# A hybrid encoder layer: transposes of the normalisation moved behind the state update, S5 regrouped, GLU second in the tail

## The chip, the cores and the metric

One Trainium2 chip, of which one core is used. The time is the device time of one launch in microseconds (us). The core has five engines, each with its own queue of instructions that it works off in order: TensorE (PE, matmuls and transposes, with a loader for weights, PEld), VectorE (DVE), ScalarE (ACT), GpSimd (POOL) and SyncE (SP), which here issues the DMAs. Matmuls write into PSUM, which has eight banks; the other engines empty them into SBUF.

## The reference

One layer over 1,152 rows (1,024 of a prompt, and 8 streams of 16 new rows) of 1,024 columns. A single projection feeds four branches, which are gated, projected, merged, projected again and normalised.

```python
def trunk_layer(x, p, rel_bias, st):
    h = split_cols(x @ p['w_in'])
    ya = s5_branch(h['a_u'], p, st)       # 32 groups, 64 complex states each; GELU, then GLU
    yb = dsa_branch(h, rel_bias, st)      # top-k attention
    yc = gdn_branch(h, p, st)             # gated DeltaNet
    yd = gla_branch(h, p, st)             # gated linear attention
    branches = stack(y_i * silu(gate_i))
    proj = einsum('ntbw,bwd->ntbd', branches, p['w_branch'])
    mixed = sum(sigmoid(merge) * proj) @ p['w_out']
    return layer_norm(DN_ALPHA * x + mixed)

def gdn_block_step(s, xs):                # one chunk of 64 rows
    ...                                   # v_new by a triangular solve, from k, v, beta, s
    o = exp(gc) * (q @ s) + (q @ k.T * dec) @ v_new
    s = exp(g_last) * s + (k * exp(g_last - gc)).T @ v_new
    return s, o                           # then rms_norm(o) * norm

def s5_branch(u, p, st):
    ...                                   # h_t = a * h_(t-1) + B u_t, complex
    y = real(C h_t) + d * u
    g = gelu(y) @ p['s5_w_glu']
    return g[..., :512] * sigmoid(g[..., 512:])
```

## The kernel before

The rows are worked on in nine tiles of 128 (tile 8 is the eight streams). Projections run in three passes of 32-bit matmuls per product (`mm3`, L189 to L191), 128 x 384 outputs at a time; their outputs are named `pg` (the input projection, its `merge` columns among them), `mix` (a branch's output projection), `glu` and `fin`. DeltaNet (`gdn_tile`) and GLA (`gla_scan`) carry a state S from tile to tile. In a DeltaNet tile the order is: triangular blocks `m`, `u`, `x` through ScalarE and VectorE, `kq`, the products `ks` and `qs` with the state, `vn`, `oi`; then `o` is normalised (`rms_gate`: squares on ScalarE, a Newton root on VectorE, `o` scaled at L1063), transposed on TensorE into `py` (L1066), gated and stored; then the state update `S` (L1025, added at L1030).

S5 goes in eight parts of four groups (`s5_part`). A part builds its matrices on VectorE (`bs`, `cs`, `AB` L1541 to L1543, `OM`), multiplies (`im`, `sx`, `kk`), fills the step matrix `TD` by DMA through DRAM, rotates (`cross`, L1584, half on VectorE and half on GpSimd), scans (L1589), writes the states `HS`, steps the eight sample streams (L1603 to L1608), multiplies again (`s5y`, L1617 and L1618), applies GELU and stores.

The tail runs the branches' `mix` in the order b, c, GLU, a, d, then `fin`. Of branches' inputs (`yl`, split into YH and YL by L112 and L113) four tiles exist; the GLU keeps two gate tiles (`glgt`, L1734).

The order on every engine is static. A list scheduler sets it when the kernel is built, from its own cost model and from priorities: recurrent chains, loads of branch inputs and the like are recorded as urgent, projections and `mix` as filler, and filler goes where an urgent instruction isn't ready by the scheduler's reckoning. `TensorE` then works this order off strictly. PSUM is in three pools: `pg` with 2 banks, `pn` with 2, and `pm` with 4, from which `m`, `u`, `kq`, `ks`, `qs`, `vn`, `oi`, `py` and `S` take theirs in turn.

## Time and profile before

| | |
|---|---|
| median of 3 runs | 1908.05 us (1903.02 to 1910.44) |
| profiled execution | 1909.76 us, span 1908.0 us |
| mean granted clock of TensorE | 0.982 of full |
| busy: TensorE, VectorE, ScalarE, GpSimd | 95%, 76%, 35%, 14% |
| attention, and DeltaNet's preparation beside S5 parts 0 and 1 | 0 to 1055 us |
| DeltaNet tiles 0 to 7 | 1055 to 1278 us |
| sample tile, rest of S5, GLA's decays | 1278 to 1420 us |
| GLA | 1420 to 1675 us |
| rest of GLU, mix of a and d | 1675 to 1800 us |
| `fin` and layer norm | 1800 to 1908 us |

Busy shares are over the whole span. A stretch is read by its own row: its busy time, and the waits of TensorE in it, by the line that waited and what released it. The profiled execution is 1.7 us above the median.

### The profile page before, as it was taken

The page shows a single profiled execution, that of the slowest core. Times are in us where ns is not written, and L with a number is a line of the kernel's source. Part 1 is how long each engine was busy: PE and PEld are TensorE (multiplying, and loading weights), DVE is VectorE, ACT ScalarE, POOL GpSimd, SP SyncE. Part 2 cuts the span into 40 slices and gives each one's busy share as a digit, 9 for nine tenths or more (in the row PEclk, how much of TensorE's full clock was granted, in tenths as well). Part 3 has the DMA queues.
Part 4 walks back from the last instruction along what each step waited for, and adds up shares of the span by engine and source line. Part 5 has one row for each costly group of instructions (what it writes and reads, how often), then busy time and mean ns, then how long its engine had stood idle before and what let it go on. Part 6 is the DMA issues. An engine that isn't in the chain of part 4 may idle for free.

```text
span 1908.0 us, 31158 instructions
## 1 busy us (share of the span) xinstructions
PE 1804.6 (95%) x10962; PEld 1710.1 (90%) x10962; DVE 1447.6 (76%) x3914; ACT 670.9 (35%) x1535; POOL 270.9 (14%) x297
## 2 busy tenths in 40 slices
PE   8999999999999999998989989899898999979997
PEld 7989999999989999997889888888888998979986
DVE  6289999944999997368890279976657899857776
ACT  4261211233666656245321333332373233222200
POOL 1110222111222210101211112211232000000000
PEclk9999999999999999999999899999999999989999
DMA  6322322232323212467335545444455673376422
GB/s 192 99 67 74 89 90 84 90 101 86 96 75 84 69 55 67 115 214 232 102 96 136 160 134 144 139 134 128 123 166 166 188 173 104 109 229 188 143 88 89
DMA packets 345290, 234.54 MB, mean 123 GB/s; under 512 B 82891, under 2 KB 327419, under 8 KB 345134
## 3 DMA queue, kind: packets, MB, share of 16 engines
q1 hardware_dynamic: 337262, 220.88, 40.1%
q10 hardware_dynamic: 7488, 10.62, 1.5%
q8 instruction: 87, 1.43, 0.3%
q0 software_dynamic: 384, 1.05, 0.2%
q14 instruction: 69, 0.57, 0.1%
HBM read 156.12 MB, written 76.35 MB: 122 GB/s over the span
## 4 chain that ended last, share of the span: by engine, by line
PE 39%; DVE 13%; DMA 5%; issue 3%; ACT 2%; POOL 1%; SPq 1%; DVEq 0%; POOLq 0%; ACTq 0%
PE pg L190 4%; PE pg L191 4%; PE pg L189 4%; PE mix L189 3%; PE mix L190 3%; PE mix L191 3%; PE fin L191 2%; PE fin L190 2%; PE fin L189 2%; PE lv L1209 1%; PE glu L191 1%; PE glu L190 1%; PE glu L189 1%; DMA S<-in_state_gdn 1%; DVE pb L870 1%
## 5 line engine op out<-in xcount | busy, mean ns | idle before, releaser
L189 PE MATMUL pg<-XH,whi 128*128 128x384 f32 x1648 | 564.0, 342 | 0.9 <-DVE gth L238 0.9
L190 PE MATMUL pg<-XL,whi 128*128 128x384 f32 x1648 | 564.3, 342 | 0.0
L191 PE MATMUL pg<-XH,wlo 128*128 128x384 f32 x1648 | 563.4, 342 | 0.0
L189 PEld LDWEIGHTS pg<-XH,whi 128*128 128x128 f32 x1648 | 312.7, 190 | 5.2 <-issue 1.8
L191 PEld LDWEIGHTS pg<-XH,wlo 128*128 128x128 f32 x1648 | 312.5, 190 | 4.1 <-issue 2.0
L190 PEld LDWEIGHTS pg<-XL,whi 128*128 128x128 f32 x1648 | 312.6, 190 | 3.1 <-issue 1.1
L109 ACT CAST whi<-wst 128x1024 fp32r<-128x1024 f32 (+2 forms) x121 | 109.5, 907 | 253.6 <-PE pg L190 118.1
L110 POOL TENSOR_TENSOR wlo<-wst,whi 128x1024 fp32r<-128x1024 f32 x44 | 109.6, 2492 | 335.3 <-ACT whi L109 329.6
L189 PE MATMUL mix<-YH,whi 128*128 128x384 f32 x384 | 132.7, 347 | 13.1 <-ACT YH L112 9.4
L110 DVE TENSOR_TENSOR wlo<-wst,whi 128x512 fp32r<-128x512 f32 (+2 forms) x77 | 76.4, 993 | 77.5 <-ACT whi L109 76.6
L190 PE MATMUL mix<-YL,whi 128*128 128x384 f32 x384 | 131.9, 344 | 1.1 <-DVE YL L113 1.1
L191 PE MATMUL mix<-YH,wlo 128*128 128x384 f32 x384 | 131.9, 344 | 0.0
L1684 ACT ACTIVATE mth<-pg 128x384 f32<-128x384 f32 x96 | 46.7, 487 | 138.3 <-PE pg L191 95.6
L392 DVE TENSOR_SCALAR_CACHE_REDUCE tkj<-mk,tk_c 128x384 bf16<-128x384 f32 (+6 forms) x112 | 90.9, 875 | 0.6
L392 DVE TENSOR_SCALAR_CACHE_REDUCE tkj<-tkh,tk_c 128x384 bf16<-128x384 bf16 (+6 forms) x112 | 90.9, 876 | 0.5
L189 PEld LDWEIGHTS mix<-YH,whi 128*128 128x128 f32 x384 | 73.4, 192 | 15.2 <-ACT YH L112 10.0
L190 PEld LDWEIGHTS mix<-YL,whi 128*128 128x128 f32 x384 | 73.3, 191 | 1.6 <-DVE YL L113 1.5
L191 PEld LDWEIGHTS mix<-YH,wlo 128*128 128x128 f32 x384 | 73.3, 191 | 0.0
L715 DVE SCALAR_TENSOR_TENSOR cy<-rb,cw,cy 128x384 f32<-128x384 f32 (+1 forms) x108 | 71.2, 659 | 2.8 <-ACT cy L713 2.2
L535 ACT ACTIVATE pr<-pr,sm 128x256 f32<-128x256 f32 (+7 forms) x72 | 53.7, 747 | 13.7 <-DVE sm L534 13.5
L1785 DVE SCALAR_TENSOR_TENSOR mth<-mth,mix 128x384 f32<-128x384 f32 x72 | 39.0, 549 | 24.1 <-PE mix L191 12.0
L502 POOL TENSOR_TENSOR mb<-BT,mk 128x512 f32<-128x512 f32 (+1 forms) x32 | 42.8, 1340 | 97.9 <-DVE mx L529 94.7
(630 smaller groups left out, 3794.9 us busy)
## 6 DMA issues: line engine op xcount, KB each, us to landing
wst<-in_w_in SPq DMA_DIRECT2D x80, 512.0 KB
wst<-in_w_branch SPq DMA_DIRECT2D x32, 256.0 KB
gk<-cq SPq DMA_DIRECT2D x27, 256.0 KB
merge_b<-mth SPq DMA_DIRECT2D x24, 192.0 KB
...
```

The source lines that it names most:

```text
L109: nc.scalar.copy(hi, src)
L110: (eng or nc.vector).tensor_tensor(lo, src, hi.bitcast(F32), op=OP.subtract)
L189: nc.tensor.matmul(ps, lh, rh, start=start, stop=False)
L190: nc.tensor.matmul(ps, lh, rl, start=False, stop=False)
L191: return nc.tensor.matmul(ps, ll, rh, start=False, stop=stop)
L392: nc.vector.tensor_scalar(junk[a % 2][:, :ns[a]], up[a] if bit > 15 else sc[a], cand[:, a:a + 1].bitcast(F32), None, op0=OP.is_ge, op1=OP.add,
L502: bias = nc.gpsimd.tensor_tensor(mbv, bt[:, 2 * jj:2 * jj + 2, ::-1][:, :, 256 - band:], mk[:, None, off:n].to_broadcast([128, 2, band]), ...
L535: nc.scalar.activation(p[:, r, 0:n], p[:, r, 0:n], AF.Exp, bias=sm[:, 2 + r:3 + r], scale=1.0, accum_out=sm[:, r:r + 1])
L715: nc.vector.scalar_tensor_tensor(yc, rb[:, i:i + c], K.cw[:, i * 12 + a:i * 12 + a + 1], yc, op0=OP.mult, op1=OP.add)
L870: nc.vector.tensor_tensor(pb[:, lo:bs, 0:lo], ab[:, j, lo:bs, None].to_broadcast([n, bs - lo, lo]), xb[:, j, None, 0:lo].to_broadcast([n, ...
L1684: nc.scalar.activation(th[:, :n], ps, AF.Tanh, scale=0.5)
L1785: nc.vector.scalar_tensor_tensor(th, th, 1.0, ps, op0=OP.add, op1=OP.mult)
```

## The change

- PSUM: after the attention the pool of 4 banks is closed; a pool of 3 takes its place, and one bank of its own holds `py`.
- `rms_gate` is called after the state update in DeltaNet and GLA, and its transposes stand later on TensorE.
- DeltaNet tile: U has two buffers, R and tmp their own, and the sample tile uses buffers of X and `at`.
- S5 part: B's six VectorE operations become three on twice the width, C's two become one; powers are kept in the order in which AB reads them; `TD` is filled by four DMAs from a zero-padded SBUF tile instead of one to DRAM and eight back; both halves of `cross` are on VectorE; HS is written by the last addition itself; the steps of the sample streams are done once for all groups before and after the parts; GELU has one VectorE operation fewer.
- The tail's order is b, GLU, c, a, d.

```diff
@@ -72,8 +72,9 @@
     K.pg = ctx.enter_context(tc.tile_pool(name="pg", bufs=2, space=PSUM))
-    K.pm = ctx.enter_context(tc.tile_pool(name="pm", bufs=4, space=PSUM))
     K.pn = ctx.enter_context(tc.tile_pool(name="pn", bufs=2, space=PSUM))
+    K.pm4 = ExitStack()
+    K.pm = K.pm4.enter_context(tc.tile_pool(name="pm", bufs=4, space=PSUM))
     c = K.const
@@ -894,9 +895,7 @@
     rd, ro, ad, zx, zu = K.GT[i]
-    X = tp.tile([128, 512], F32, tag="X", name="X")
-    U = tp.tile([128, 512], F32, tag="U", name="U")
-    nc.sync.dma_start(X, zx)
+    U = tp.tile([128, 512], F32, tag="U", name="U", bufs=2)
     nc.sync.dma_start(U, zu)
@@ -920,6 +919,8 @@
+        X = tp.tile([128, 512], F32, tag="X", name="X")
+        nc.sync.dma_start(X, zx)
@@ -968,8 +969,8 @@
     nc.vector.tensor_tensor(kdec, v4(pk), bc(kd), op=OP.mult)
-    R = tp.tile([128, 4, 128], F32, tag="L", name="R")
-    tmp = tp.tile([128, 4, 128], F32, tag="M", name="tmp")
+    R = tp.tile([128, 4, 128], F32, tag="R", name="R")
+    tmp = tp.tile([128, 4, 128], F32, tag="tmp", name="tmp")
     if i < 8:
@@ -1018,7 +1020,6 @@
             nc.vector.scalar_tensor_tensor(o[:, h], po[:, H4[h]], rq[:, h:h + 1], tmp[:, h], op0=OP.mult, op1=OP.add)
-    rms_gate(K, o, K.gnorm, gt, tp, "c", s)
     if i < 8:
@@ -1049,6 +1050,7 @@
+    rms_gate(K, o, K.gnorm, gt, tp, "c", s)
@@ -1061,7 +1063,7 @@
     nc.vector.tensor_tensor(o, o, bc(ss), op=OP.mult)
-    py = pmt(K, "py")
+    py = K.pr.tile([128, 512], F32, tag="py", name="py")
     for h in range(4):
@@ -1282,7 +1284,6 @@
         nc.vector.tensor_tensor(o, pov, oi, op=OP.add)
-    rms_gate(K, o, K.dnorm, gt, tp, "d", s)
     if i < 8:
@@ -1320,6 +1321,7 @@
+    rms_gate(K, o, K.dnorm, gt, tp, "d", s)
@@ -1403,12 +1405,16 @@
     new = lambda n, s=(128, 32): c.tile(list(s), F32, name=n)
-    K.PR, K.PI = new("PR", (128, 9, 32)), new("PI", (128, 9, 32))
     K.WR, K.WI = new("WR"), new("WI")
...
@@ -1507,47 +1513,45 @@
...
-    co = lambda x: x[:, gs, None].to_broadcast([128, 4, 16])
-    t = tl("bt", (4, 16))
-    bs1, bs2 = tl("bs1", (4, 16)), tl("bs2", (4, 16))
-    nc.vector.tensor_tensor(bs1, b1, co(K.CR), op=OP.mult)
-    nc.vector.tensor_tensor(t, b2, co(K.CIS), op=OP.mult)
-    nc.vector.tensor_tensor(bs1, bs1, t, op=OP.add)
-    nc.vector.tensor_tensor(bs2, b2, co(K.SCR), op=OP.mult)
-    nc.vector.tensor_tensor(t, b1, co(K.NCI), op=OP.mult)
-    nc.vector.tensor_tensor(bs2, bs2, t, op=OP.add)
...
+    nc.vector.tensor_tensor(bs, bb, co(K.C1), op=OP.mult)
+    nc.vector.tensor_tensor(t, bb[:, ::-1], co(K.C2), op=OP.mult)
+    nc.vector.tensor_tensor(bs, bs, t, op=OP.add)
+    bs1, bs2 = bs[:, 0], bs[:, 1]
...
-    cs1, cs2 = tl("cs1", (4, 16)), tl("cs2", (4, 16))
-    v = lambda ap: ap.rearrange("p (g c) -> p g c", g=4)
-    nc.vector.tensor_scalar(cs1, v(ps[:, 0:64]), K.sgn, None, op0=OP.mult)
-    nc.vector.tensor_scalar(cs2, v(ps[:, 64:128]), -1.0, None, op0=OP.mult)
+    cs = tl("cs1", (2, 4, 16))
+    nc.vector.tensor_tensor(cs, ps[:, 0:128].rearrange("p (x g c) -> p x g c", x=2, g=4),
+                            K.sg2[:, :, None, None].to_broadcast([128, 2, 4, 16]), op=OP.mult)
+    cs1, cs2 = cs[:, 0], cs[:, 1]
...
-    AB, tmp = tl("AB", (4, 16, 8)), tl("big", (4, 9, 16))[:, :, 0:8].rearrange("p g s c -> p g c s")
-    pa = lambda x: pw(x, 0, 8)[:, :, None, :].to_broadcast([128, 4, 16, 8])
+    AB, tmp = tl("W", (4, 16, 8)), tl("big", (4, 16, 9)).rearrange("p g c s -> p (g c s)")[:, 0:512].rearrange(
+        "p (g c s) -> p g c s", g=4, c=16)
+    pa = lambda x: K.PW[:, x, gs, None, 1:9].to_broadcast([128, 4, 16, 8])
     ea = lambda x: x[:, :, :, None].to_broadcast([128, 4, 16, 8])
-    rv = AB[:, :, :, ::-1]
-    nc.vector.tensor_tensor(rv, pa(K.PR), ea(bs1), op=OP.mult)
-    nc.vector.tensor_tensor(tmp, pa(K.PI), ea(bs2), op=OP.mult)
-    nc.vector.tensor_tensor(rv, rv, tmp, op=OP.add)
+    nc.vector.tensor_tensor(AB, pa(0), ea(bs1), op=OP.mult)
+    nc.vector.tensor_tensor(tmp, pa(1), ea(bs2), op=OP.mult)
+    nc.vector.tensor_tensor(AB, AB, tmp, op=OP.add)
     OM, tmp = tl("OM", (4, 9, 16)), tl("big", (4, 9, 16))
...
     nc.vector.tensor_tensor(OM, OM, tmp, op=OP.add)
-    IM = tl("IM", (4, 128))
+    IM = tl("G", (4, 128))
     pi = pnt(K, "im")
@@ -1560,7 +1564,7 @@
-    kz = tl("kz", (4, 8, 16))[0:16]
+    kz = K.kz[:, :, 112:240].rearrange("p g (t c) -> p g t c", t=8)
@@ -1569,45 +1573,33 @@
     nc.vector.tensor_tensor(kz[:, :, 0], kz[:, :, 0], dg, op=OP.add)
-    kd = K.dram.tile([16, 4, 128], F32, name=f"kz{q}")
-    nc.sync.dma_start(kd, kz.rearrange("p g s c -> p g (s c)"))
-    for s in range(8):
-        nc.sync.dma_start(TD[s::8, :, s * 16:128], kd[:, :, 0:128 - s * 16])
+    for g in range(4):
+        nc.sync.dma_start(TD[:, g], bass.AP(tensor=K.kz.tensor, offset=K.kz.offset + g * 240 + 112,
+                                            ap=[[list(K.kz.ap[0])[0], 16], [-16, 8], [1, 128]]))
     CO, SI = (x[:, g0 % 16:g0 % 16 + 4] for x in (K.CO, K.SI))
...
-        for a, eng in ((0, nc.vector), (64, nc.gpsimd)):
+        for a in (0, 64):
             r = slice(64 - a, 128 - a)
-            eng.tensor_tensor(dst[a:a + 64], src[r], SI[r], op=OP.mult)
+            nc.vector.tensor_tensor(dst[a:a + 64], src[r], SI[r], op=OP.mult)
     cross(W, SX[:, :, 0:128])
...
     nc.vector.tensor_tensor(G, G, W, op=OP.subtract)
+    h1 = K.HH[:, gs, :, 1]
+    sx = SX[:, :, 128:144].rearrange("p g (b a) -> p g b a", a=2)
+    nc.vector.tensor_tensor(h1, h1, sx[:, :, :, 0], op=OP.add)
+    nc.vector.tensor_copy(HS[:, :, 128:144], K.HH[:, gs].rearrange("p g b a -> p g (b a)"))
+    nc.vector.tensor_copy(K.HF[:, 1:9, gs].rearrange("p b g -> p g b"), sx[:, :, :, 1])
     for g in range(4):
...
     nc.vector.tensor_tensor(W, W, CO, op=OP.mult)
-    nc.vector.tensor_tensor(W, W, G, op=OP.add)
-    nc.gpsimd.memset(HS[:, :, 0:1], 0.0)
-    nc.vector.tensor_copy(HS[:, :, 1:128], W[:, :, 0:127])
-    nc.vector.tensor_copy(K.HF[:, 0, gs], W[:, :, 127])
-    f8, t8 = tl("f8", (4, 8)), tl("t8", (4, 8))
-    hs, sx = (x[:, :, 128:144].rearrange("p g (b a) -> p g b a", a=2) for x in (HS, SX))
-    b8 = lambda x: x[:, 8, gs, None].to_broadcast([128, 4, 8])
-
-    def step(out, h, x):
-
-        nc.vector.tensor_tensor(t8[0:64], h[64:128], b8(K.PI)[64:128], op=OP.mult)
-        nc.vector.scalar_tensor_tensor(t8[64:128], h[0:64], -1.0, b8(K.PI)[0:64], op0=OP.mult, op1=OP.mult)
-        nc.vector.tensor_tensor(f8, h, b8(K.PR), op=OP.mult)
-        nc.vector.tensor_tensor(f8, f8, t8, op=OP.subtract)
-        nc.vector.tensor_tensor(out, f8, x, op=OP.add)
-    nc.vector.tensor_copy(hs[:, :, :, 0], K.H0[:, gs])
-    step(hs[:, :, :, 1], K.H0[:, gs], sx[:, :, :, 0])
-    step(K.HF[:, 1:9, gs].rearrange("p b g -> p g b"), hs[:, :, :, 1], sx[:, :, :, 1])
+    nc.vector.tensor_tensor(HS[:, :, 1:128], W[:, :, 0:127], G[:, :, 0:127], op=OP.add)
+    nc.vector.tensor_tensor(K.HF[:, 0, gs], W[:, :, 127], G[:, :, 127], op=OP.add)
     Y = tl("Y", (4, 144))
@@ -1618,18 +1610,33 @@
     z = tl("big", (4, 9, 16)).rearrange("p g t c -> p (g t c)").rearrange("p (g k) -> p g k", g=4)
-    nc.scalar.activation(z, Y, AF.Square)
-    nc.vector.tensor_scalar(z, z, 0.044715, 1.0, op0=OP.mult, op1=OP.add)
-    nc.vector.tensor_tensor(z, z, Y, op=OP.mult)
+    nc.scalar.activation(z, Y, AF.Square, scale=math.sqrt(0.044715))
+    nc.vector.scalar_tensor_tensor(z, z, 1.0, Y, op0=OP.add, op1=OP.mult)
     nc.scalar.activation(z, z, AF.Tanh, scale=math.sqrt(2 / math.pi))
...
@@ -1663,7 +1675,10 @@
             TD = p1.tile([128, 4, 128], F32, name="TD")
-            nc.gpsimd.memset(TD, 0.0)
+            K.kz = p1.tile([16, 4, 240], F32, name="kz")
+            nc.gpsimd.memset(K.kz[:, :, 0:112], 0.0)
+            K.HS = p1.tile([128, 4, 144], F32, name="HS")
+            nc.gpsimd.memset(K.HS[:, :, 0:1], 0.0)
             for q in range(8):
@@ -1793,8 +1808,8 @@
         mix_branch(K, 0, "b", yp, p)
-        mix_branch(K, 1, "c", yp, p)
-        s5_glu(K, 2, yp, p)
+        s5_glu(K, 1, yp, p)
+        mix_branch(K, 2, "c", yp, p)
         mix_branch(K, 3, "a", yp, p)
@@ -1992,6 +2007,9 @@
                     dsa(K, between)
+            K.pm4.close()
+            K.pm = ctx.enter_context(tc.tile_pool(name="pm3", bufs=3, space=PSUM))
+            K.pr = ctx.enter_context(tc.tile_pool(name="pr", bufs=1, space=PSUM))
             if "c" in stages:
...
             gdn_conv_state(K)
```

How the order moves. On TensorE at the end of DeltaNet tile 0 (names as above; `pg` are projection matmuls), before:

```order
L1014 MATMUL oi<-VN,P 128x128 x4
L190 MATMUL pg<-XL,whi 128x384
L191 MATMUL pg<-XH,wlo 128x384
...
L190 MATMUL pg<-XL,whi 128x384
L1066 MATMUL py<-ident,o 128x128 x4
L1025 MATMUL S<-VN,kdec 128x128 x4
L933 MATMUL m_12498<-X,L 64x64 x4
```

and in the same place after:

```order
L1016 MATMUL oi<-VN,P 128x128 x4
L1026 MATMUL S<-VN,kdec 128x128 x4
L934 MATMUL m_12505<-X,L 64x64 x4
...
L956 MATMUL u_12532<-U,M 64x64 x4
L960 MATMUL kq<-kq 128x128 x3
L1068 MATMUL py<-ident,o 128x128 x4
L960 MATMUL kq<-kq 128x128
L964 MATMUL pv<-ident,vt 128x128 x4
```

The 43 filler matmuls between `oi` and `py` are gone, S follows `oi` at once, and `py` stands in the next tile, among its `kq`. Between the state updates of tile 1 and tile 7 there were 375 filler matmuls and are 195; S5's fell from 72 to 33. Of the five groups of GLA's diagonal matmuls (`diag`, the first for the sample tile, one for each pair of tiles), the second to the fifth had 637 fillers (`pg`, `mix` and `glu`) between them and have 297. VectorE's order between the same state updates holds instructions for 172 us at their durations of before, and now 122 us; between the same diagonals 178 and 109 us (the sums count the overlap of neighbours twice).

On SyncE at the end of the GLU (`glgt` a gate, `y_a` the branch's result in DRAM, `yl` the load of a branch's input), before:

```order
L1738 DMA y_a<-glgt 128x384
L1756 DMA yl<-y_a 128x4x384 x2
L182 DMA wst<-in_w_branch 128x4x128
L1734 DMA glgt<-gate_a 128x384
L1780 DMA mth<-merge_a_95 128x384
L1738 DMA y_a<-glgt 128x384
...
L1756 DMA yl<-y_a 128x4x384
```

and after:

```order
L1753 DMA y_a<-glgt 128x384
L1795 DMA mth<-merge_c_111 128x384
L1771 DMA yl<-y_a 128x4x384
L1749 DMA glgt<-gate_a 128x384
L183 DMA wst<-in_w_branch 128x4x128
L1753 DMA y_a<-glgt 128x384
L1795 DMA mth<-merge_c_111 128x384 x2
```

The loads of `y_a` still follow its stores closely, but on TensorE the 288 matmuls of branch c now lie between the GLU and branch a, whose first matmul reads them.

## Rows read from the trace of the kernel before

Columns of the stretches, from the left: stretch, its length, busy us (and instructions) of PE, PEld, DVE, ACT and POOL, granted clock of TensorE, share of the DMA engines, GB/s. Columns of instructions by line: line, engine, operation, out<-in, shape, count, then busy us, mean ns, idle us before. In a timeline, square brackets hold the engine's idle time before the instruction and what released it.

**Rows 1.** Page, part 1: engine, busy us (share of span) and instructions.
```profile
PE 1804.6 (95%) x10962; PEld 1710.1 (90%) x10962; DVE 1447.6 (76%) x3914; ACT 670.9 (35%) x1535; POOL 270.9 (14%) x297
```

**Rows 2.** Busy time by stretch: dense projections, then the start of DeltaNet.
```profile
1000.00:1050.00 50.00, 50.00 (x290) 50.00 (x289) 2.59 (x8) 9.94 (x19) 9.57 (x4) 1.00 0.49 134
1050.00:1100.00 50.00, 45.70 (x306) 41.85 (x305) 14.10 (x44) 16.59 (x52) 8.18 (x8) 0.86 0.56 161
```

**Rows 3.** Same view: six DeltaNet tiles, then three pairs of GLA tiles.
```profile
1111.40:1274.80 163.40, 148.62 (x1103) 135.55 (x1102) 147.14 (x429) 58.62 (x174) 36.96 (x31) 0.99 0.48 140
1459.40:1626.60 167.20, 158.09 (x961) 152.61 (x959) 152.05 (x359) 53.75 (x121) 5.91 (x7) 0.98 0.57 156
```

**Rows 4.** Waits of TensorE, 1055 to 1278: line, releaser, total us, times, longest.
```profile
PE py L1066 <- DVE o L1063: 8.7, 5, 4.2
PE im L1553 <- DVE AB L1543: 5.4, 3, 2.3
...
PE qs L983 <- DVE P L960: 2.2, 2, 1.1
```

**Rows 5.** Timeline at the end of DeltaNet tile 3: start us, duration us.
```profile
1148.74 0.72 PE L1014 MATMUL oi<-VN,P 128*128 128x128 f32 x5
...
1162.76 0.66 PE L1066 MATMUL py<-ident,o 128*128 128x128 f32 x4 [0.69 <-DVE o L1063]
1163.25 0.94 PE L1025 MATMUL S<-VN,kdec 128*128 128x128 f32 x7
...
1172.05 0.69 DVE L960 TENSOR_TENSOR P<-kq,P 128x512 f32<-128x512 f32 x1 [0.25 <-PE kq L959]
```

**Rows 6.** Waits of TensorE, 825 to 1055.
```profile
PE s5y L1617 <- DVE HF L1596: 2.6, 1, 2.6
PE s5y L1617 <- DVE HS L1595: 2.4, 1, 2.4
```

**Rows 7.** Waits of TensorE, 1420 to 1710.
```profile
PE mix L189 <- ACT YH L112: 9.4, 2, 8.6
...
PE mix L189 <- DVE mth L1785: 3.2, 3, 2.2
PE mix L190 <- DVE YL L113: 1.1, 1, 1.1
```

**Rows 8.** Timeline between GLU and branch a.
```profile
1684.30 0.32 SPq L1738 DMA_DIRECT2D y_a<-glgt  x1
...
1687.52 1.33 SPq L1756 DMA_DIRECT2D yl<-y_a  x2
...
1692.01 1.48 ACT L112 ACTIVATE YH<-yl 128x1536 fp32r<-128x1536 f32 x1 [6.58 <-DMA yl<-y_a]
...
1693.54 0.69 PE L189 MATMUL mix<-YH,whi 128*128 128x384 f32 x1 [8.64 <-ACT YH L112]
```

**Rows 9.** Instructions by line, S5: VectorE 825 to 1420, TensorE in the six tiles.
```profile
L1541 DVE TENSOR_TENSOR AB<-PR,bs 128x512 f32<-128x512 f32 x8 | 10.6, 1322 | 0.0
...
L1584 DVE TENSOR_TENSOR G<-W,SI 64x512 f32<-64x512 f32 x8 | 9.5, 1182 | 0.2
...
L1584 DVE TENSOR_TENSOR W<-SX,SI 64x512 f32<-64x512 f32 x8 | 7.5, 933 | 0.2
...
L1603 DVE TENSOR_TENSOR t<-HS,PI 64x32 f32<-64x32 f32 x8 | 4.8, 598 | 0.2
...
L1622 DVE TENSOR_SCALAR big<-big 128x576 f32<-128x576 f32 x8 | 5.6, 695 | 4.1 <-ACT big L1621 4.0
...
L1587 DVE TENSOR_TENSOR G<-G,W 128x512 f32<-128x512 f32 x8 | 5.4, 677 | 0.0
...
L1561 PE MATMUL sx<-UT,IM 128*128 128x144 f32 x28 | 5.2, 335 | 0.0
```

**Rows 10.** Timeline: one GpSimd instruction and a VectorE one beside it.
```profile
1146.83 2.38 POOL L110 TENSOR_TENSOR wlo<-wst,whi 128x1024 fp32r<-128x1024 f32 x1 [5.62 <-PE pg L191]
...
1147.14 2.39 DVE L1622 TENSOR_SCALAR big<-big 128x576 f32<-128x576 f32 x1
```

More of the change, by code (lines that the diff above doesn't have):

```diff
@@ L987, in gdn_tile @@
     else:
-        kqT = tp.tile([128, 4, 2, 128], F32, tag="kqT", name="kqT")
+        kqT = [tp.tile([128, 4, 128], F32, tag=t, name="kqT") for t in ("X", "at")]
         s8 = lambda nm, h: nm.rearrange("b h k v -> k h b v")[:, h]
@@ L996, in gdn_tile @@
                 nc.tensor.matmul(pk[:, b * 32:b * 32 + 32], S8[:, b], kq[:, :, h, t16], start=True, stop=True)
-            nc.scalar.copy(kqT[:, h].rearrange("p a (b t) -> p b a t", b=8),
-                           pk[:, 0:256].rearrange("p (b a t) -> p b a t", b=8, a=2))
+            for a in range(2):
+                nc.scalar.copy(kqT[a][:, h].rearrange("p (b t) -> p b t", b=8),
+                               pk[:, 0:256].rearrange("p (b a t) -> p b a t", b=8, a=2)[:, :, a])
         pks = pmt(K, "ks")
@@ L1405, in s5_params @@
     new = lambda n, s=(128, 32): c.tile(list(s), F32, name=n)
-    K.PR, K.PI = new("PR", (128, 9, 32)), new("PI", (128, 9, 32))
     K.WR, K.WI = new("WR"), new("WI")
-    K.R8, K.CR, K.CIS, K.SCR, K.NCI = new("R8"), new("CR"), new("CIS"), new("SCR"), new("NCI")
-    K.sgn = new("sgn", (128, 1))
+    K.PW = new("PW", (128, 2, 32, 9))
+    K.PR, K.PI = (K.PW[:, x, :, ::-1].rearrange("p g k -> p k g") for x in range(2))
+    K.R8 = new("R8")
+    K.C1, K.C2 = new("C1", (128, 2, 32)), new("C2", (128, 2, 32))
+    K.CR, K.SCR, K.CIS, K.NCI = K.C1[:, 0], K.C1[:, 1], K.C2[:, 0], K.C2[:, 1]
+    K.sg2 = new("sg2", (128, 2))
+    K.sgn = K.sg2[:, 0:1]
+    nc.vector.memset(K.sg2, -1.0)
     nc.vector.memset(K.sgn[0:64], 1.0)
-    nc.vector.memset(K.sgn[64:128], -1.0)
     K.hpi = new("hpi", (128, 1))
@@ L1640, in s5_states_in @@
             nc.tensor.transpose(ps[:, x * 128:x * 128 + 128], h.rearrange("p d s -> p (d s)"), K.ident)
-        nc.vector.tensor_copy(K.H0.rearrange("p g b -> p b g"), ps[:, 0:256].rearrange("p (b g) -> p b g", b=8))
+        nc.vector.tensor_copy(K.HH[:, :, :, 0].rearrange("p g b -> p b g"),
+                              ps[:, 0:256].rearrange("p (b g) -> p b g", b=8))
+        s5_chunk(K, K.HH[:, :, :, 1], K.HH[:, :, :, 0], None,
+                 [p.tile([128, 32, 8], F32, name=n) for n in ("s5f", "s5u")])
 def s5_states_out(K):
@@ L1646, in s5_states_out @@
     with tc.tile_pool(name="s5o", bufs=1) as p:
+        x = K.HF[:, 1:9].rearrange("p b g -> p g b")
+        s5_chunk(K, x, K.HH[:, :, :, 1], x, [p.tile([128, 32, 8], F32, name=n) for n in ("s5f", "s5u")])
         f = K.HF.rearrange("p b g -> p (b g)")
```

29 lines of the change are left out of this document (22 added, 7 removed).

## The prediction

> **What bounds the kernel now.** First the engines: TensorE is busy for 1804.6 of 1908.0 us, VectorE for 1447.6 [rows 1]. The matmuls of before and after are the same work, so the time can change only by what TensorE waits: some 103 us without a record, and what hides in slow records. Then the stretches. Where projections run alone there is no wait: 290 matmuls fill 50.00 us at the full clock, 172 ns each [rows 2]. In the six DeltaNet tiles of rows 3 a tile takes 163.40 / 6 = 27.2 us, with TensorE busy for 148.62 / 6 = 24.8 us and VectorE for 147.14 / 6 = 24.5 us: two engines that both nearly fill the tile, and each stands for 2.4 to 2.7 us of it. GLA reads the same: a pair takes 167.20 / 3 = 55.7 us, TensorE 52.7, VectorE 50.7 [rows 3]. So in both recurrent stretches filler is needed to hide VectorE's work, and as long as both engines carry the same load, less work on VectorE alone would only let the scheduler put less filler there. That is what the orders show it doing.
>
> Third, the waits. Of TensorE's in the DeltaNet stretch the largest is `py` for the normalised `o`: 8.7 us in five of eight tiles, then `im` for AB with 5.4 us [rows 4]. In the timeline `oi` ends at 1149.5, `py` starts at 1162.76 after a wait of 0.69 us, and `S` at 1163.25 [rows 5]. So the state update, which needs nothing of `py`, stands 13.8 us behind `oi`. That is no idle time: filler runs in it.
>
> **The change part by part.** The profiled execution took 1909.8 us (span 1908.0), 1.7 above the median; the sum is made against it.
>
> 1. *Normalisation behind the update, DeltaNet.* Between the updates of tiles 1 and 7 fillers fall from 375 to 195, so 30 a tile, 30 x 0.172 = 5.2 us; S5's matmuls fall from 72 to 33, 6.5 a tile, each of two records of 5.2 / 28 = 0.186 us [rows 9], 2.4 us. TensorE's tile becomes 24.8 - 7.6 = 17.2 us. VectorE's falls by the ratio 122 / 172 of its order, to 24.5 x 0.71 = 17.4 us. Its part of this comes from S5: three parts now stand ahead of the tiles instead of two, and a part is shorter (below). The two engines stay level, so I take the same relative loss as in rows 3: 27.2 / 24.8 = 1.097, a tile of 17.4 x 1.097 = 19.1 us and 1.9 us of it without TensorE, where it was 2.4. Over the seven steps that is -4 us. The fillers that leave are not gained: they run elsewhere at 172 ns. Bounds: if VectorE runs with no gap, the tile takes 17.4 us and TensorE loses 0.2 a tile (-15 us over seven); if `py` waits at its new place, +19 us (second rival).
>
> 2. *The same in GLA.* 340 fillers fewer in three pairs: 113 x 0.172 = 19.5 us, TensorE's pair 33.2 us; VectorE's 50.7 x 109 / 178 = 31.0 us. With the ratio 55.7 / 52.7 = 1.057 the loss falls from 3.0 to 1.9 us a pair, over four pairs -4 us. Bounds: no loss, -12; the loss of today, 0.
>
> 3. *S5 part.* At one part: the steps of the sample streams go (L1603 alone 0.598 us of a dozen small ones), the scale of GELU (0.695), half of `bs`; the AB operation, 1.322 us with its strided reading, has 512 elements as L1587 with 0.677 us has, and I take the middle; against this the two halves of `cross` come over from GpSimd, and cost VectorE 1.182 and 0.933 us as their twins do [rows 9]. Together some 4 us less in a part of 22 us. This is VectorE time and is in the ratios of 1 and 2. On TensorE: before the tiles `s5y` waited 2.6 and 2.4 us for HF and HS [rows 6], and HS now comes from one addition and not a sum and a copy: -5; a third part ahead of the tiles meets one more wait for AB, 5.4 / 3 = +1.8 [rows 4]. -3 in all. The DMAs that fill TD from SBUF are not in the trace; the nearest rows bound them: no wait at all, or the 2.4 us that `s5y` waits once, in each of the eight parts (+19). I take 0, since the matmuls with TD stand behind the whole rotation.
>
> 4. *GpSimd out of `cross`.* While GpSimd works on 1024 columns (2.38 us from 1146.83), a VectorE operation issued at 1147.14 takes 2.39 us and ends at 1149.53 [rows 10], where its mean is 0.695 [rows 9]. The sixteen pieces of `cross` on GpSimd leave. The Trainium skill, page "SBUF — State Buffer", section "Who interferes with whom", says that the two engines share a port pair which one instruction holds whole while the other stops. The trace agrees, with those 2.39 us. By that rule each of the sixteen pieces could stop VectorE as this one did, for 2.39 - 0.695 = 1.7 us, 27 us in all, and their move, which by the rows adds 8 x (1.182 + 0.933) = 17 us to VectorE, would cost nothing; the sum would be some 2 us lower. I leave that out.
>
> 5. *Tail.* `yl` of branch a is issued at 1687.52, behind the last stores of the GLU; YH follows at 1692.01 and TensorE, which has nothing else, starts 1.5 us later after 8.64 us of waiting [rows 8]. Of this kind rows 7 hold 9.4 and 1.1 us. In the new order 288 matmuls of branch c, 288 x 0.172 = 50 us, stand between the GLU and branch a. They cover the 9.2 us from the store (1684.30) to the first matmul (1693.54) five times: -10.5. What is late next: the gate loads, two buffers for twelve of them, and `mth` at a branch's start, 3.2 / 3 = 1.1 us each [rows 7]; with two more starts in a stretch without other work, +2. So -8. If the cover fails, because SyncE queues the loads of c's `mth` behind `yl`, that wait comes at the start of c and nothing is gained.
>
> Sum: -4 - 4 - 3 - 8 = -19, or 1891 for the profiled execution and, 1.7 lower, 1889 for a median; I say 1890.
>
> **Rivals.**
>
> *More than that (1866).* Once `S` follows `oi` at once and VectorE has less to do, the recurrent chain is no longer late anywhere, and TensorE's loss in the tiles goes to the lower bounds: -15 - 12 - 5 - 10.5 = -43. For it: the gap of 13.8 us between `oi` and `S` [rows 5] was all filler, and the order now has none there. Against: VectorE has never been without gaps in these stretches [rows 3], and it serves S5, DeltaNet and the normalisation in one queue.
>
> *No change (1913).* `py` waits in its new place. In the old order it came 13.3 us after `oi` and still waited [rows 5]. In the new one TensorE reaches it with `kq`; from `S` at 1163.25 to the `kq` that releases L960 at 1172.05 is 8.8 us, about 9.5 from the end of `oi`. If VectorE takes as long for `o` as now, with S5's instructions between its steps, `py` waits 13.3 - 9.5 = 3.8 us a tile, 2.7 more than today's 8.7 / 8 = 1.1, so +19 over seven tiles where I have -4; with -4 for GLA, -3 and -8 the sum is +4, 1914. For it: the wait of 4.2 us in rows 4. Against: in the new order less of S5 lies between.
>
> *Slower (1943).* Three PSUM banks for the chain instead of four. A group of matmuls then waits until VectorE or ScalarE has emptied the third bank back, not the fourth. The price is that of `qs`, which waits 1.1 us for L960 to empty the bank of `kq` [rows 4]. About six such groups a tile (`kq`, `ks`, `qs`, `vn`, `oi`, `S`) would make 6 x 1.1 x 8 = 53 us; 1909.8 - 19 + 53 = 1944. It decides from (19 + 10) / 8 = 3.6 us a tile on. For it: the order now packs `oi`, `S` and `m` without filler, which is where a bank is emptied. Against: `py` no longer takes one of the ring.
>
> *Slower by the clock (1930).* In the first 50 us of the DeltaNet stretch TensorE was busy for 45.70 us and the granted clock 0.86, between its two levels; in the tiles it was 0.99 [rows 2, 3]. Should the thinner stretches be granted 0.86, their work of 7 x 17.2 + 4 x 33.2 = 253 us grows by 253 x (0.99 / 0.86 - 1) = 38 us: 1910 - 19 + 38 = 1929. The Trainium skill, page "TensorE: Matmul & The Clock Gate", section "A second HAM failure mode: psum-queue depth-cycling", tells of a kernel whose clock went up and down because of short idle times as it cycled through PSUM banks. The tiles at 0.99 with 9% of idle time speak against it here.
>
> **How the numbers follow.** Forecast 0.40, more 0.17, no change 0.20, slower by banks 0.16, by the clock 0.07. A measurement of this kernel tells about 0.5% from no change, so faster means under 1898.5 and slower over 1917.6. Faster: 0.17, and 0.35 of the 0.40 (its terms could be off by 8 us), 0.52 in all. Same: 0.05 of the forecast, 0.16 of no change, 0.02 of a weak case of the banks, 0.23. Slower: 0.25. The range runs from 1856, ten under the largest gain, to 1935, which takes in the clock and the lighter cases of the banks. The forecast's own range is 1880 to 1900.
>
> **What would show it.** Right: tiles between the updates of 19 to 20 us, GLA pairs of about 35; no wait of `mix` for YH over 1 us between GLU and a; `s5y` no longer waiting for HS. Wrong: a wait of `py` for L1063 of 3 us or more in most tiles; waits of `ks`, `qs`, `vn` or `m` for VectorE or ScalarE that sum to over 3.6 us a tile; a granted clock under 0.95 in the tiles; waits for TD.

## The result, and the profile after

The changed kernel takes 1883.5 us (median of 4 runs, 1880.6 to 1888.4) against 1905.5 us for the kernel before, run beside it: the ratio is 0.9884 with a 95% interval of 0.9852 to 0.9917. The forecast was 1890 us. The profiled execution spans 1882.5 us at a mean granted clock of 0.987. The engines, as in [rows 1]:

```profile
PE 1797.8 (95%) x10962; PEld 1704.2 (91%) x10962; DVE 1419.2 (75%) x3827; ACT 670.8 (36%) x1539; POOL 244.6 (13%) x274
```

VectorE has 28 us less to do, TensorE as many instructions as before. The stretches that answer to [rows 3], six DeltaNet tiles between two state updates and three GLA pairs between their diagonals (columns as there):

```profile
1088.50:1196.50 108.00, 103.87 (x852) 94.56 (x851) 94.88 (x327) 47.53 (x153) 16.08 (x14) 1.00 0.59 171
1372.30:1480.00 107.70, 98.73 (x616) 92.15 (x614) 98.59 (x247) 37.70 (x100) 15.53 (x13) 0.97 0.31 94
```

A tile takes 108.0 / 6 = 18.0 us where 27.2 were needed and 19.1 forecast; a pair takes 35.9 us where 55.7 were needed and 35.1 forecast. TensorE is busy in 96% of the tiles now (91% before), but in 92% of the pairs (95% before). The waits of TensorE around the tiles, as in [rows 4]:

```profile
PE m L934 <- DMA S<-in_state_gdn: 3.2, 1, 3.2
PE py L1068 <- DVE o L1065: 2.8, 2, 2.3
PE m L951 <- ACT X L945: 2.5, 3, 1.6
...
PE im L1557 <- DVE W L1547: 0.9, 1, 0.9
```

The normalised `o` is waited for twice only, 2.8 us in all, of which 2.3 in the sample tile, and none of the chain's groups shows a wait for a PSUM bank. Ahead of the tiles, as in [rows 6], `s5y` still waits for HS and HF, 5.9 us against 5.0:

```profile
PE s5y L1609 <- DVE HS L1601: 3.6, 2, 2.1
...
PE s5y L1609 <- DVE HF L1602: 2.3, 1, 2.3
```

From the last GLA pair to `fin`, which answers to [rows 7]:

```profile
PE mix L190 <- DVE ACC L1798: 5.2, 1, 5.2
PE lv L1211 <- DVE X L1206: 4.3, 2, 2.2
PE mix L190 <- DVE mth L1800: 1.9, 2, 1.3
```

The wait of 9.4 us for branch a's YH is gone. A new one stands in front: the first `mix` of branch b that finds no PSUM bank, since VectorE hasn't added the earlier ones to ACC. Its origin is read on three engines (SyncE, VectorE, TensorE):

```profile
1525.60 0.50 SPq L1229 DMA_DIRECT2D dgt<-gate_d  x1
```

```profile
1525.06 0.68 DVE L1065 TENSOR_TENSOR glo<-glo,oss 128x512 f32<-128x512 f32 x1
1530.41 0.75 DVE L1070 SCALAR_TENSOR_TENSOR oyt<-py,dnorm,dgt 128x512 f32<-128x512 f32 x1 [4.67 <-DMA dgt<-gate_d]
1531.08 1.47 DVE L1798 SCALAR_TENSOR_TENSOR ACC<-mth,mix 128x384 f32<-128x384 f32 x3
```

```profile
1531.68 0.69 PE L190 MATMUL mix<-YH,whi 128*128 128x384 f32 x1 [5.16 <-DVE ACC L1798]
```

The last GLA tile's gate is issued at 1525.60, because its only buffer is free once the tile before has been gated. The gating (L1070) waits for it from 1525.74 to 1530.41, the additions to ACC stand behind it in VectorE's queue, and TensorE waits for them until 1531.68. The ten microseconds from 1530 on are granted 0.73 of the clock, a mean of its two levels, and the next ten all of it:

```profile
1530.00:1540.00 10.00, 8.32 (x38) 8.32 (x39) 4.43 (x9) 0.62 (x1) 0.00 (x0) 0.73 0.81 250
1540.00:1550.00 10.00, 10.00 (x59) 10.00 (x58) 3.37 (x6) 0.62 (x1) 0.00 (x0) 1.00 0.59 178
```

Where the 25.5 us of the two profiled spans went is seen when each stretch's time is set against the work in it. The work is the count of matmuls in the order by their durations in dense rows (172 ns for 128 x 384, as in [rows 2], and in the same way for the other shapes); the rest is TensorE's loss, clock included. It is an estimate: with other durations for the small shapes a cell moves by up to 3 us, and a difference between two columns by about 1. GLA begins here with the diagonals of the sample tile. In us:

| stretch | before | after | bank alone | S5 alone | all but S5 | S5 and tail |
|---|---|---|---|---|---|---|
| to the update of tile 0 | 93.7 | 88.7 | 93.3 | 82.8 | 86.7 | 83.4 |
| tiles 0 to 7 | 35.1 | 15.5 | 20.6 | 33.1 | 20.0 | 28.5 |
| sample tile, S5, decays | 21.9 | 17.8 | 57.0 | 12.2 | 44.4 | 11.5 |
| GLA to the last diagonals | 26.8 | 26.8 | 46.5 | 39.0 | 54.0 | 43.8 |
| to GLA's last transposes | 3.1 | 9.7 | 13.2 | 5.8 | 14.2 | 8.9 |
| to `fin` | 15.6 | 12.2 | 27.1 | 16.8 | 3.5 | 1.9 |

The last four columns are experiments; "all but S5" is the kernel with the S5 branch put back.

### The profile page after: what moved, and what is told of

It reads as the page before. It is cut to its first block, busy times and chain, and to the rows that moved or that the text cites. A ratio compares the mean times of both kernels' runs of the same rounds, so it can differ in the third digit from the quotient of the medians.

```text
span 1882.5 us, 31013 instructions
## 1 busy us (share of the span) xinstructions
PE 1797.8 (95%) x10962; PEld 1704.2 (91%) x10962; DVE 1419.2 (75%) x3827; ACT 670.8 (36%) x1539; POOL 244.6 (13%) x274
## 5 line engine op out<-in xcount | busy, mean ns | idle before, releaser
L192 PE MATMUL fin<-WOH,YL 128*128 128x512 f32 x144 | 56.1, 389 | 0.0
```

Of the source, the lines that this page charges most:

```text
L192: return nc.tensor.matmul(ps, ll, rh, start=False, stop=stop)
```

## The experiments

Ratios are to the kernel before on the same chip, with 95% intervals; 0.01 is 19 us.

**The DeltaNet call put back** (the changed kernel with one line moved):

```diff
@@ gdn_tile @@
+    rms_gate(K, o, K.gnorm, gt, tp, "c", s)
     if i < 8:
         pS = pmt(K, "S")
...
-    rms_gate(K, o, K.gnorm, gt, tp, "c", s)
```

> The changed kernel with one edit undone: in the DeltaNet tiles the normalisation is called before the state update again (its transposes keep their own PSUM bank; GLA stays changed). The changed kernel lost 15.5 us of TensorE's time between the updates of tiles 0 and 7, the kernel before 35.0. Theory A, the gain of 19.5 us is the place of the transposes: most of it goes, the time rises by 12 to 19 us, and TensorE waits for the normalised o at the transposes again, 0.5 to 1 us a tile or more. Theory B, the gain is the shorter S5 part on VectorE: the time rises by under 5 us and the loss between the updates stays below 21 us.

Ratio 0.9981 (0.9961 to 1.0000), some 18 us above the changed kernel, which looks like theory A. It is not: the loss in the tiles is 19.4 us, and the kernel with two gate buffers, whose order in the tiles is that of the changed kernel, has 20.0 on the same chip. The order in the tiles is the same with the call in either place. Theory B's bound on the loss holds, its bound on the time doesn't. The time went elsewhere. Against that neighbour, whose profiled span is 19.3 us shorter, 7.7 us lie between GLA's last transposes and `fin`, and some 6.6 in GLA, 5.0 of them in the three pairs (22.5 against 17.5). Behind GLA TensorE waits as follows:

```profile
PE mix L190 <- DVE ACC L1798: 12.3, 1, 12.3
PE mix L190 <- DVE mth L1800: 1.1, 1, 1.1
```

On SyncE and VectorE in the same place (start, duration):

```profile
1536.18 5.35 SPq L1726 DMA_DIRECT2D gy<-s_y  x6
1541.57 0.99 SPq L1300 DMA_DIRECT2D out_p_gla<-glS  x1
1542.61 0.59 SPq L1071 DMA_DIRECT2D y_d<-oyt  x1
1543.25 1.53 SPq L1795 DMA_DIRECT2D mth<-merge_b  x3
```

```profile
1546.24 1.23 DVE L1798 SCALAR_TENSOR_TENSOR ACC<-mth,mix 128x384 f32<-128x384 f32 x2 [8.06 <-DMA mth<-merge_b]
```

Loads of the GLU's input (`gy`), which the tail's new order has moved up, hold up SyncE, the merge loads of branch b come behind them, and the additions to ACC start at 1546.24.

**The S5 branch put back** (the functions from `s5_params` to `s5` are those of before):

> The changed kernel with the S5 branch of the kernel before (its parameters, parts, DMAs through DRAM, half of the rotation on GpSimd and its steps); everything else changed. Theory A (place of the transposes): the time rises by 3 to 8 us, of which some 3 to 5 stand ahead of the DeltaNet tiles, and the loss between the updates of tiles 0 and 7 stays under 21 us. Theory B (shorter S5 part): it rises by 12 us or more, and the loss between the updates goes back to about 30 us.

Ratio 1.0155 (1.0128 to 1.0183). Without the new S5 the rest of the change makes the kernel slower. Theory B's size is passed by far, but not where it put it: the tiles lose 20.0 us as their neighbours do. The loss is in the stretch behind the tiles and in GLA (table).

**The tail's old order:**

```diff
-        s5_glu(K, 1, yp, p)
-        mix_branch(K, 2, "c", yp, p)
+        mix_branch(K, 1, "c", yp, p)
+        s5_glu(K, 2, yp, p)
```

> The changed kernel with the tail's old order b, c, GLU, a, d. By the prediction the wait of branch a's first matmul for its input comes back, about 9 us and its neighbours, so the time rises by 8 us or more. The rival: GLU groups and branch c stand under the last GLA pair again and cover its waits, where the changed kernel lost 10.9 us between the last diagonals and the last transposes against 3.3 before; then the two cancel and the time moves by under 3 us either way.

Ratio 0.9954 (0.9935 to 0.9972): 0.0070, some 13 us, above the changed kernel. The prediction's 8 us hold, the rival falls: the loss from the last diagonals to GLA's last transposes is 9.9 us with the old order and 9.7 with the new. The waits of 9.4 and 1.1 us of [rows 7] are nearly all back:

```profile
PE mix L190 <- ACT YH L113: 7.6, 2, 6.3
PE mix L190 <- DVE mth L1800: 7.2, 1, 7.2
...
PE mix L191 <- DVE YL L114: 1.1, 1, 1.1
```

**Two buffers for GLA's gate:**

```diff
-    gt = tp.tile([128, 4, 128], F32, tag="dgt", name="dgt", bufs=1)
+    gt = tp.tile([128, 4, 128], F32, tag="dgt", name="dgt", bufs=2)
```

> The changed kernel with two buffers instead of one for the gate tile of GLA. In the changed kernel the last tile's gating waits 4.67 us for its gate's load, since the buffer is free only after the tile before has been gated; the additions to ACC stand behind it on VectorE, and TensorE waits 5.16 us for them. Theory: that wait goes, and with it the stretch of granted clock 0.73 behind it (2.7 us in 10): the time falls by 5 to 8 us. The rival: another release comes as late (the gating's own transposes, or the load of the merge columns), and it falls by under 2 us.

Ratio 0.9859 (0.9827 to 0.9890), 5 us below the changed kernel, though the intervals overlap. The wait for the gate is gone, but another comes almost as late, the load of the merge columns; TensorE's wait shrinks from 5.16 to 4.46 us, so the rival's mechanism is what the trace shows:

```profile
1533.61 0.69 PE L190 MATMUL mix<-YH,whi 128*128 128x384 f32 x1 [4.46 <-DVE ACC L1798]
```

**The bank alone** (the kernel before, with a bank for `py` and a ring of three; calls not moved):

```diff
+            K.pm4.close()
+            K.pm = ctx.enter_context(tc.tile_pool(name="pm3", bufs=3, space=PSUM))
+            K.pr = ctx.enter_context(tc.tile_pool(name="pr", bufs=1, space=PSUM))
...
-    py = pmt(K, "py")
+    py = K.pr.tile([128, 512], F32, tag="py", name="py")
```

> The kernel before with one edit: the transposes of the normalisation get a PSUM bank of their own and the ring shrinks to three banks. The calls stay in their old place, S5 and the tail too. In its order the state update follows oi at once all the same, and between the updates of tiles 0 and 7 there are some 105 us of TensorE's work, as in the changed kernel, where the kernel before has 158. Theory C: the bank alone sets that order, and it is worth nothing by itself, since the old S5 then runs on alone behind the tiles and uses up the fillers that GLA needs, as with the changed kernel on the old S5 (1.0155 of before): the time is 1 to 3% above before. The rival, theory A in its new form: the bank is the gain in the tiles, and the time falls by 10 us or more.

Ratio 1.0323 (1.0297 to 1.0348), the slowest of all. Its order shows what sets the place of the update, since the call stands where it did:

```
L1015 MATMUL oi<-VN,P 128x128 x4
L1026 MATMUL S<-VN,kdec 128x128 x4
```

And its stretches show what became of it: six tiles, from there to the first diagonals, three pairs (columns as above):

```profile
1087.70:1196.10 108.40, 103.01 (x834) 93.07 (x833) 87.92 (x285) 47.39 (x153) 19.23 (x18) 0.97 0.58 163
1196.10:1444.60 248.50, 214.27 (x1221) 200.70 (x1219) 161.50 (x387) 81.56 (x151) 62.74 (x53) 0.94 0.41 115
1475.20:1587.10 111.90, 91.38 (x524) 85.63 (x522) 100.54 (x253) 35.37 (x94) 7.31 (x9) 0.86 0.43 129
```

```profile
1196.50:1346.60 150.10, 142.59 (x871) 132.13 (x869) 110.12 (x255) 66.35 (x127) 29.70 (x35) 1.00 0.53 148
```

The tiles take 18.1 us, in the changed kernel 18.0. The stretch behind them takes 248.5 us where the changed kernel (last row) takes 150.1. TensorE is kept busy there for 214 us, but with fillers (883 of them, where the changed kernel has 563), and those are then lacking in GLA: the three pairs have 209 against 297, and TensorE is busy for 91 of 111.9 us, at a clock of 0.86. The chain in that stretch is S5's, where TensorE waits longest for HS:

```profile
PE s5y L1618 <- DVE HS L1596: 13.2, 3, 4.8
```

So theory C holds, with a larger price than it gave.

**The new S5 alone** (the functions from `s5_params` to `s5` of the changed kernel in the kernel before):

> The kernel before with the new S5 branch alone (old banks, old calls, old tail). Its order has the fillers between oi and the transposes as before. Theory C (the two need each other): the tiles lose as much as before, and what S5 saves on VectorE brings little, the time falls by under 8 us. The rival, theory B: the shorter S5 is most of the gain by itself, and the time falls by 12 us or more.

Ratio 0.9967 (0.9944 to 0.9990), 6 us. Theory C's bound holds; theory B falls. By the table the loss is some 23 us smaller up to GLA's first diagonals and some 16 larger behind them. GLA's part of that isn't explained: the three pairs keep 552 fillers of 637.

**Both calls put back**, DeltaNet's and GLA's, the bank kept:

> The changed kernel with both calls of the normalisation back ahead of the state updates; the bank of its own, S5 and the tail stay changed. Its order between the updates is that of the changed kernel. Theory: the place of the calls is worth nothing in the tiles (loss between the updates of tiles 0 and 7 within 2 us of the 20 us that its neighbours on this chip have); the time differs from the changed kernel only by what the seam between GLA and branch b does, where with only DeltaNet's call put back TensorE waited 12.3 us for ACC. The rival: the place of GLA's call matters, the pairs lose over 5 us more, as the kernel with DeltaNet's call alone put back did (22.5 against 17.5).

Ratio 0.9966 (0.9947 to 0.9984). The tiles lose 20.1 us and the pairs 19.5 (17.5 with two gate buffers): in both the place of the call is worth next to nothing, and the rival falls. But the kernel is 16 us above the changed one. Against the kernel with two gate buffers, whose profiled span is 20.9 us shorter, 9.6 us are the loss behind GLA (TensorE waits 12.1 us for ACC again), 5.8 us the sample tile with S5 and the decays; the second part the theory had not named.

**The GLU's input from another queue**, together with two gate buffers:

```diff
-                nc.sync.dma_start(y[:, k].rearrange("p (s t) -> p s t", s=8),
+                nc.gpsimd.dma_start(y[:, k].rearrange("p (s t) -> p s t", s=8),
```

> The changed kernel with two gate buffers and, beside them, the twelve loads of the GLU's input (gy) issued from GpSimd's queue instead of SyncE's. With the GLU second in the tail these twelve stand on SyncE ahead of the merge loads of branch b, take 7.66 us for eight of them and wait for buffers; b's first additions wait up to 3 us each for their merge load, TensorE 4.5 us for ACC. Theory: the merge loads come in time, that wait goes and the clock behind it stays up: 4 to 8 us less than with two gate buffers alone. The rival: the DMA engines are full there (0.9 and more of their time), so the loads land as late as now, and the time moves by under 2 us.

Ratio 0.9835 (0.9801 to 0.9869), the fastest kernel here, below the changed one and the one with two gate buffers. From the last transposes to `fin` the loss falls from 10.7 us to 3.8, and no wait for ACC is left:

```profile
PE py L1068 <- DVE glo L1065: 0.8, 1, 0.8
PE mix L190 <- DVE mth L1800: 0.8, 1, 0.8
```

The ten microseconds from 1530 on are granted all of the clock, where with two gate buffers alone they were granted 0.66. The rival falls: the DMA engines were busy (0.91 to 0.97 of their time from 1500 to 1530), but the loads were late by their place in SyncE's queue. Against two gate buffers alone the timed gain is 0.0024, inside the intervals; the wait that went is what shows the cause.

**Everything but the bank** (`py` from a ring of four again):

> The changed kernel without the bank of its own: the transposes of the normalisation take theirs from the ring, which has four banks again; the moved calls, the new S5 and the new tail stay. Its order has 150 us of TensorE's work between the updates of tiles 0 and 7, as the kernel before has 158, and not 109. By the pair with the old tail (new S5 alone 0.9967 of before, everything but the tail 0.9954) the bank is worth next to nothing once S5 is short. Theory D: S5 and the tail are the gain and the bank is neutral, so this kernel is within 0.4% of the changed one (0.9884). The rival, theory E: the bank is what lets the tail pay, since it leaves GLA the fillers under which the GLU stood before; then this kernel is at 0.994 to 1.000.

Ratio 0.9904 (0.9881 to 0.9927), within 0.2% of the changed kernel, though its tiles lose some 31 us by the measure of the table, where the changed kernel loses 15.5. Theory D holds.

**A ring of two banks:**

```diff
-            K.pm = ctx.enter_context(tc.tile_pool(name="pm3", bufs=3, space=PSUM))
+            K.pm = ctx.enter_context(tc.tile_pool(name="pm3", bufs=2, space=PSUM))
```

> The changed kernel with a ring of two PSUM banks for the recurrent chains instead of three. In the prediction a ring shorter by a bank was priced at 6 groups x 1.1 us a tile, 53 us. That price right: the time rises by 40 us or more and TensorE shows waits of ks, qs, vn, oi or S for VectorE or ScalarE of 1 us each. The rival: a bank is emptied long before it is needed again, since the chain itself waits for each step, and the time rises by under 15 us, without such waits.

Ratio 0.9926 (0.9896 to 0.9956), 8 us above the changed kernel, though the intervals overlap. The rival holds. In the tiles no group of the ring waits for a bank to be emptied: `u` and `m` wait for operands, and `kk`, the one that may wait for a bank, has it from another pool:

```profile
PE u L941 <- ACT MZ L938: 2.0, 2, 1.1
PE m L951 <- ACT X L945: 1.5, 4, 0.6
PE kk L1570 <- DVE SX L1566: 1.4, 1, 1.4
PE im L1557 <- DVE W L1547: 0.6, 1, 0.6
```

Two things limit this. The profiled execution is the shortest of six (1883.5 us; the longest took 1899.4), so its trace doesn't show where the 8 us of the median lie. And the scheduler made another order for the shorter ring, with 228 fillers between the updates of tiles 1 and 7 where the changed kernel has 195.

**Half of `cross` back on GpSimd:**

```diff
-        for a in (0, 64):
+        for a, eng in ((0, nc.vector), (64, nc.gpsimd)):
             r = slice(64 - a, 128 - a)
-            nc.vector.tensor_tensor(dst[a:a + 64], src[r], SI[r], op=OP.mult)
+            eng.tensor_tensor(dst[a:a + 64], src[r], SI[r], op=OP.mult)
```

> The changed kernel with half of each rotation's cross products back on GpSimd. In the trace of the changed kernel VectorE's halves take 0.686 and 0.930 us each, where they took 0.933 and 1.182 us beside their twins on GpSimd. Theory (the two engines hold each other up): VectorE's halves go back to about 0.93 and 1.18, VectorE saves only 8 x (0.686 x 2 - 0.933 + 0.930 x 2 - 1.182) = 9 us over all parts, and a part gets longer by the slower of the twins, 1.4 to 1.5 us against 2 x 0.686 and 2 x 0.930: the time stays within 0.3% of the changed kernel. The rival: VectorE is what paces S5's parts, and the time falls by 6 us or more.

Ratio 1.0066 (1.0045 to 1.0087), some 35 us above the changed kernel. Both expectations are wrong. By their means VectorE's halves do get longer, one of them to 1.162 us, and GpSimd's take 1.4 to 1.5:

```profile
L1587 DVE TENSOR_TENSOR W<-SX,SI 64x512 f32<-64x512 f32 x8 | 9.3, 1162 | 0.3
...
L1587 DVE TENSOR_TENSOR G<-W,SI 64x512 f32<-64x512 f32 x8 | 7.6, 949 | 0.3
```

```profile
L1587 POOL TENSOR_TENSOR G<-W,SI 64x512 f32<-64x512 f32 x8 | 12.0, 1496 | 33.8 <-DVE W L1597 13.0 <-PE S L1048 9.6 <-DVE rs_y L658 7.6
L1587 POOL TENSOR_TENSOR W<-SX,SI 64x512 f32<-64x512 f32 x8 | 11.5, 1439 | 77.6 <-DVE SX L1566 48.7 <-DVE rows L841 14.5 <-DVE dg L1574 12.4
```

The means mix two cases, which the timeline of the two engines tells apart:

```profile
927.35 1.27 POOL L1587 TENSOR_TENSOR W<-SX,SI 64x512 f32<-64x512 f32 x1 [14.46 <-DVE rows L841]
927.46 1.71 DVE L1587 TENSOR_TENSOR W<-SX,SI 64x512 f32<-64x512 f32 x1
...
1115.78 0.69 DVE L1587 TENSOR_TENSOR W<-SX,SI 64x512 f32<-64x512 f32 x1
1115.89 1.71 POOL L1587 TENSOR_TENSOR W<-SX,SI 64x512 f32<-64x512 f32 x1 [2.64 <-DVE SX L1566]
```

The half that begins first takes its own time, 0.69 us on VectorE and 1.27 on GpSimd. The other one, if it begins while that one runs, ends late: VectorE's 0.55 us after GpSimd's has ended, and GpSimd's after 1.7 us. Nor does VectorE have less to do in this kernel: it is busy for 1422.6 us, with all of `cross` for 1419.2.

Ahead of the tiles TensorE waits 7.7 us for HS in place of 3.6:

```profile
PE s5y L1609 <- DVE HS L1601: 7.7, 2, 4.1
```

By stretches the loss is 8 us larger ahead of the tiles, 2 in them, 9 behind them, 8 at the head of GLA and 12 behind it. The first and third hold S5; how the others come from it was not tried, but their order is another one too. Between the last diagonals and GLA's last transposes it is 3 us smaller.

**S5 and the tail alone** (the kernel before with these two edits):

> The kernel before with the new S5 and the new order of the tail, and nothing else: four banks in the ring, the calls of the normalisation and the buffers in the tiles as before. So far, as ratios to before: new S5 alone 0.9967, everything but the tail 0.9954, everything but the bank 0.9904, everything 0.9884. Theory D: these two edits are the gain, 0.988 to 0.992. The rival: the moved calls and buffers of the tiles carry a part of it, and the time is at 0.994 to 0.998.

Ratio 0.9917 (0.9890 to 0.9944). Theory D holds: these two are most of the gain, and the rest of the change adds 0.003, which the intervals don't tell from nothing. The tail alone on the kernel before was not run.

## Why the prediction was right, and where not

The direction and the size of the whole were right, by a sum whose terms were not.

1. *Normalisation behind the update, DeltaNet (-4).* The step that failed. The tiles lost 35.1 us and lose 15.5, so this term came to -19.6, beyond the forecast's lower bound of -15; five kernels with the same order in the tiles lose 18 to 21 us on other chips, which makes it -14 to -17. In the prediction's own measure, the time in which TensorE isn't busy, a tile has (108.00 - 103.87) / 6 = 0.7 us, where 1.9 were forecast. The premise that failed is that the two engines stay level: TensorE's work in a tile came as forecast, 17.3 us against 17.2, but VectorE's came to 15.8 against 17.4, and the loss per tile did not stay in proportion. Whether VectorE's lighter tile or `S` right behind `oi` keeps TensorE from being late there isn't told apart, since both come with the bank's order. But it is no gain of the kernel's: the bank alone has the same tiles and is 3.2% slower, and everything but the bank is within 0.2% of the whole. The mechanism was misnamed as well. The call's place does nothing to the order in the tiles; the bank does. And the sentence that the fillers which leave "run elsewhere at 172 ns" is the root of it. They do that only if there is an elsewhere. With the old S5 they were spent behind the tiles, under a chain that took 248 us, and GLA then ran short of them.

2. *The same in GLA (-4).* 0. Pairs of 35.9 us were near the forecast (35.1), the loss up to the last diagonals stayed at 26.8 us: the upper bound. VectorE's work in a pair fell to 32.9 us and not to 31.0, level with TensorE's 32.9, and 3.0 us of a pair are without TensorE, as before. Behind the last diagonals the loss grew by 6.6 us, which no step held. There are 136 fillers there where there were 190, but S5 and the tail alone has 228 and loses 8.9 us, so that this is the cause isn't shown.

3. *S5 part (-3).* Its direct term was wrong (5.9 us of waits for HS and HF against 5.0; the loss ahead of the tiles fell by 5 all the same), and its real worth was not in the sum. Alone it gives 6 us; in the changed kernel, where S5's rest lies bare behind the tiles, 52 us hang on it. VectorE's saving was sized well: 28.4 us over eight parts, 3.6 each against 4. But three of its prices were means that hold an operation stopped by GpSimd: AB's 1.322 us is seven operations of 1.03 to 1.10 and one of 3.15 beside GpSimd's split of a weight, L1622's 0.695 is seven of 0.44 to 0.46 and the 2.39 of [rows 10], and L1603's 0.598 is 0.19 in most. AB was put in the middle between 0.677 and 1.322 us and went to the lower end, 0.683:

```profile
L1587 DVE TENSOR_TENSOR G<-W,SI 64x512 f32<-64x512 f32 x16 | 14.9, 930 | 0.4
...
L1587 DVE TENSOR_TENSOR W<-SX,SI 64x512 f32<-64x512 f32 x16 | 11.0, 686 | 0.4
...
L1614 DVE SCALAR_TENSOR_TENSOR big<-big,Y 128x576 f32<-128x576 f32 x8 | 7.3, 918 | 0.5 <-ACT big L1613 0.5
...
L1545 DVE TENSOR_TENSOR W<-PW,bs 128x512 f32<-128x512 f32 x8 | 5.5, 683 | 0.1
L1601 DVE TENSOR_TENSOR HS<-W,G 128x508 f32<-128x508 f32 x8 | 5.4, 680 | 0.0
```

The loads of TD from SBUF were taken at 0, and cost 1.8 us once.

4. *GpSimd out of `cross` (no number).* The means of VectorE's own halves fell from 0.933 to 0.686 and from 1.182 to 0.930 us (sixteen of each now), so by the means the move costs it 8 x (2 x 0.686 - 0.933 + 2 x 0.930 - 1.182) = 9 us and not 17. A half takes 0.69 us in each of these kernels when nothing stops it; the 0.930 holds two of 2.79 and 2.48 us, which began behind GpSimd's splits of weights:

```profile
1212.97 2.37 POOL L111 TENSOR_TENSOR wlo<-wst,whi 128x1024 fp32r<-128x1024 f32 x1 [8.93 <-ACT whi L110]
1213.41 2.48 DVE L1587 TENSOR_TENSOR G<-W,SI 64x512 f32<-64x512 f32 x1
```

So GpSimd still stops VectorE now and then. The Trainium skill, page "SBUF — State Buffer", section "Who interferes with whom", has the rule that the prediction names, one instruction holding the shared ports whole; the timelines agree, 0.69 us for the half that begins first and 1.42 to 1.80 for VectorE's half when it begins second. The prediction's second reading of that rule, that the move would cost VectorE nothing, fits better than the 17 us of its rows: VectorE is busy for 1419.2 us with all of `cross` and for 1422.6 with half. The experiment says that the move is worth about 35 us to the kernel, in the order that the scheduler made of either; those 35 us are not explained by VectorE's time.

5. *Tail (-8).* Right: 13 us by undoing it, 9.5 us between S5 alone and S5 with the tail. The cover of 50 us was enough. In the changed kernel itself the loss from the last transposes to `fin` fell only from 15.6 to 12.2 us, since a new wait came. What came late next was not the GLU's gate loads or SyncE at c's start, but SyncE at the start of b.

That the sum came out near is in good part luck. By the table, against the forecast in brackets: -5.0 us ahead of the tiles (-3), -19.6 in them (-4), -4.1 around the sample tile (nothing), +6.6 in GLA and behind it (-4), -3.4 to `fin` (-8). These errors of up to 15.6 us, two of them the other way, leave -25.5 where -19 stood.

The rivals. *More than that*: its mechanism, the chain no longer late, is what happened in the tiles, where 0.7 us a tile are left without TensorE, and not in GLA. *No change*: `py` waited 0.5 us in one of the eight tiles, not 3.8 in each. *Slower by banks*: the changed kernel with three shows no wait for a bank, and a ring of two instead of three costs some 8 us, inside the intervals, and not 53; the waits that its trace shows are for operands. *Slower by the clock*: the granted clock in the tiles was 1.00. It fell instead where TensorE had waited, to 0.73 behind the gate's load.

What stays open: why both calls in their old place cost 6 us around the sample tile, how half of the 35 us of `cross` comes about in GLA and behind it, and why GLA loses 39.0 and 43.8 us with the new S5 and the old banks, with 552 and 547 fillers in the three pairs, where the kernel before lost 26.8 with 637. The number of fillers alone doesn't set GLA's loss.
